# Attention scores in split fp32: two passes over the whole TensorE array in place of three passes of row pairs

## The chip, the core and the metric

The kernel runs on one core of a Trainium2 chip. The metric is the time of one execution on the device, in microseconds (us). The engines that matter here are TensorE (PE in the profile; PEld is its loading of stationary operands), VectorE (DVE), ScalarE (ACT) and SyncE (SP), which issues nearly all DMAs.

## The reference, cut to what matters

Two layers of a decoder trunk over 256 tokens of width 1024, all in fp32. Each layer has two attention mixers side by side and a feed-forward part. Three products of queries and keys, all with 64-wide heads, decide the scores:

```python
# DSA: an indexer scores all keys; the best 64 per token are kept
rel = jax.nn.relu(jnp.einsum('bthd,bsd->bths', iq_i, ik).astype(jnp.float32))
score = jnp.einsum('bths,bth->bts', rel, iw_i.astype(jnp.float32))
_, sel = lax.top_k(score, k_top)
...
s = jnp.einsum('bthd,btkhd->bhtk', q_i, kg) * ATTN_SCALE
...
# NSA: 8 heads in 2 groups; compressed, selected and window branches
s_s = jnp.einsum('bgrtd,bgtnkd->bgrtnk', q_i, kg)
s_w = jnp.einsum('bgrtd,bsgd->bgrts', q_i, kw) * ATTN_SCALE
...
x = x + _hybrid_mixer(...)
x = x + _swiglu(_rmsnorm(x, ffn_norm[l]), w_ffn_gate[l], w_ffn_up[l], w_ffn_down[l])
```

## The kernel before

**Split fp32.** A matmul in type f32r takes one pass, but keeps fewer bits than f32. So an fp32 value is held as a high part (rounded to f32r by ACT) and a low part (the value less its high part, by DVE), and a product of two fp32 values is three f32r matmuls: high by high, high by low, low by high. Weights go through `weights` (L155 to L167: a DMA, ACT at L164, DVE at L165) and `mul3` (L169 to L175); the activations are split once per norm.

**Scores.** One head has 64 rows, so it fills half of the array's 128 rows. Two heads (or groups) e = 0, 1 lie on rows 0 to 63 and 64 to 127 (`HALF`). `split` makes the high and low part of all 128 rows in one ACT and one DVE instruction. `pair` (L320 to L325) then issues, for each of the three products, one matmul on the upper and one on the lower 64 rows, each into a PSUM bank of its own. Per layer there are ten such blocks: two of the indexer for the second half of the tokens (256 keys wide, tiles `iqs`, `iks`), two of `nsa(0)` (256 wide) and four of `nsa(1)` (512 wide; tiles `qs`, `ks`), and two of `dsa(1)` (256 wide; tiles `dqs`, `dks`). A block of 256 columns is twelve matmuls, one of 512 columns six. The indexer and `dsa` for the first half of the tokens use plain f32 on row halves (L422, L648).

**Other tiled matmuls.** The values (L595, L636) use half of the array's columns, the compression (L505) a quarter. A plain f32 matmul shows as two in the trace.

**What sets the order.** The program is written layer by layer: indexer, NSA projections, compression, DSA projections, `nsa(0)`, `nsa(1)`, the splits of `dks` and `dqs` (L664 to L667), `dsa(0)`, `dsa(1)`, gate projections, branches, output, feed-forward. A list scheduler that simulates time then orders each engine's instructions; it mixes the attention's small matmuls into the projections that come before and after (their weights have buffers for four steps). Scores go to the two `sc` banks; both come free only when DVE has read them (L297, the first pass of `softmax`), so the next block waits for the softmax of the one before. `iks`, `ks` and `dqs` share one buffer (tag `ks`), `iqs`, `qs` and `dks` another (tag `qs`).

Of the kernel before, what the change touches and what calls it, by code (L numbers as in the profile page):

```python
# [9 lines left out]
F32 = mybir.dt.float32  # L10
F32R = mybir.dt.float32r
AF = mybir.ActivationFunctionType
# [4 lines left out]
P = 128  # L17
SEQ = 256
NT = SEQ // P
# [12 lines left out]
HALF = (slice(0, 64), slice(64, 128))  # L32
# [47 lines left out]
def hybrid_trunk(ctx: ExitStack, tc: tile.TileContext, a: dict, out: bass.AP):  # L80
    nc = tc.nc
# [5 lines left out]
    one = ctx.enter_context(tc.tile_pool(name="one", bufs=1))  # L87
# [224 lines left out]
        return pt  # L312


    def split(dst, src):

        nc.scalar.activation(dst[0], src, AF.Copy)
        nc.vector.tensor_sub(dst[1], src, dst[0].bitcast(F32))

    def pair(outs, q, k):  # L320


        for n, (a, b) in enumerate(((0, 0), (0, 1), (1, 0))):
            for e in range(2):
                nc.tensor.matmul(outs[e], q[a][HALF[e]], k[b][HALF[e]], start=n == 0, stop=n == 2)  # L325

    ALL = cst[:, K_ZERO:K_ZERO + 2 * P]

# [14 lines left out]
    for l in range(DEPTH):  # L343
# [14 lines left out]
        qT, dqT = carve(ga, 2608, 4, SEQ), carve(ga, 3632, 4, SEQ)  # L358
        accs = carve(ga, 4656, NT, SEQ)

        ks = one.tile([P, 2, NT, 2 * P], F32R, tag="ks", name="ks")
        qs = one.tile([P, 2, 4, SEQ], F32R, tag="qs", name="qs")
        ikT = carve(ga, 5168, P)
        gates = carve(gb, 0, NT, 2 * D)
# [1 line left out]
        dkT = carve(gb, 4096, 4, SEQ)  # L366
# [20 lines left out]
        iw = small.tile([P, NT, 8], F32, tag="iw", name="iw", bufs=1)  # L387
        dbias = []
        iqs = one.tile([P, 2, 4, SEQ], F32R, tag="qs", name="iqs")[:, :, :, 0:P]
        iks = one.tile([P, 2, NT, 2 * P], F32R, tag="ks", name="iks").rearrange("p a b t -> p a (b t)")[:, :, 0:SEQ]  # L390
        for i in range(NT):
            nc.vector.tensor_scalar_mul(iw[:, i], pji[:, i, 576:584], 512 ** -0.5)
            rope(pji[:, i, 0:576].rearrange("p (h d) -> p h d", d=64), i, (9,))
            nc.vector.tensor_copy(pji[:, i, 576:640], pji[:, i, 512:576])
            tok = slice(i * P, (i + 1) * P)
            qp = tr_bank()
            for k in range(4):
                nc.tensor.transpose(qp[:, k * P:(k + 1) * P], pji[:, i, k * P:(k + 1) * P], ident)
            q3 = qp.rearrange("p (k t) -> p k t", t=P)
            if i == 0:  # L400
                iqT = work.tile([P, 4, P], F32, tag="pr", name="iqT", bufs=8)
                nc.scalar.activation(iqT, q3, AF.Copy)
            else:
                split([iqs[:, a] for a in range(2)], q3)
            kp = tr_bank()[:, 0:P]
            nc.tensor.transpose(kp, pji[:, i, 512:640], ident)
            nc.scalar.activation(iks[:, 0, tok], kp, AF.Copy)
            if i == 0:
                nc.scalar.activation(ikT, kp, AF.Copy)
            nc.vector.tensor_sub(iks[:, 1, tok], kp, iks[:, 0, tok].bitcast(F32))  # L410
        for i in range(NT):
            nk = P * (i + 1)
            acc = accs[:, i, 0:nk]
            prev = causal(i)
            per = 512 // nk
            for p0 in range(0, 4, per):
                sbs = [sc_bank() for _ in range(2)]
                for p in range(p0, p0 + per):
                    outs = [sb[:, (p - p0) * nk:(p - p0 + 1) * nk] for sb in sbs]
                    if i == 0:  # L420
                        for e in range(2):
                            nc.tensor.matmul(outs[e], iqT[HALF[e], p], ikT[HALF[e]], start=True, stop=True)  # L422
                    else:
                        pair(outs, [iqs[:, z, p] for z in range(2)], [iks[:, z] for z in range(2)])
                for e in range(2):
                    rl = work.tile([P, 512], F32, tag="k2", name="rl", bufs=3)
                    nc.scalar.activation(rl, sbs[e], AF.Relu)
                    for p in range(p0, p0 + per):
                        h = 2 * p + e
                        nc.vector.scalar_tensor_tensor(acc, rl[:, (p - p0) * nk:(p - p0 + 1) * nk],  # L430
                                                       iw[:, i, h:h + 1], prev, ALU.mult, ALU.add)
                        prev = acc
            dbias.append(acc)
# [12 lines left out]
        for c0, n in ((512, 512), (1024, 280), (0, 512)):  # L446
            d = project(act, w_in, c0, n)
            for i in range(NT):
                if c0 == 0:
                    nq[i] = work.tile([P, 512], F32, tag="q2", name="nq", bufs=4)  # L450
                    evac(nq[i].rearrange("p (r g d) -> p r g d", r=4, g=2),
                         d[i].rearrange("p (g r d) -> p r g d", g=2, r=4), rstd[i])
                else:
                    evac(pj[:, i, c0 - C0:c0 - C0 + n], d[i][:, 0:n], rstd[i])
        eg = small.tile([P, NT, 24], F32, tag="eg", name="eg", bufs=1)
        kvP = work.tile([P, 2, 2, P], F32, tag="k2", name="kvP", bufs=3)
        for i in range(NT):
            rope(pj[:, i, 0:768].rearrange("p (a b d) -> p a b d", a=3, b=4)[:, :, 0:2], i, (3, 2))
            rope(nq[i].rearrange("p (h d) -> p h d", d=64), i, (8,))
            sp = tr_bank()  # L460
            for kind, c0 in ((0, C_KCMP), (1, C_VCMP)):
                for g in range(2):
                    for par in range(2):
                        o = (kind * 2 + g) * 64
                        nc.tensor.matmul(sp[par * 64:(par + 1) * 64, o:o + 64],
                                         pj[:, i, c0 - C0 + g * 64:c0 - C0 + g * 64 + 64],
                                         cst[:, K_SEL + par * 64:K_SEL + par * 64 + 64], start=True, stop=True)
            nc.vector.tensor_copy(kvP[:, :, :, i * 64:(i + 1) * 64],
                                  sp[:, 0:256].rearrange("p (k g c) -> p k g c", k=2, g=2))
            kp = tr_bank()  # L470
            for k, c in enumerate((C_KSLC, C_KWIN)):
                nc.tensor.transpose(kp[:, k * P:(k + 1) * P], pj[:, i, c - C0:c - C0 + P], ident)
            split([ks[:, z, i] for z in range(2)], kp[:, 0:2 * P])
            tok = slice(i * P, (i + 1) * P)
            qp = tr_bank()
            for r in range(4):
                nc.tensor.transpose(qp[:, r * P:(r + 1) * P], nq[i][:, r * P:(r + 1) * P], ident)
            q3 = qp.rearrange("p (r t) -> p r t", t=P)
            nc.scalar.activation(qT[:, :, tok], q3, AF.Copy)
            split([qs[:, z, :, tok] for z in range(2)], q3)  # L480
            nc.scalar.activation(eg[:, i], pj[:, i, C_NG - C0:C_NG - C0 + 24], AF.Exp, scale=-1.0)
            nc.vector.tensor_scalar(eg[:, i], eg[:, i], 1.0, None, ALU.add)

# [55 lines left out]
        for c0, dst in ((C_DQ, dqT), (C_DK, dkT), (C_DV, None)):  # L539
            d = project(act, w_in, c0, 512)  # L540
            for i in range(NT):
                if dst is None:
                    evac(dv[:, i], d[i], rstd[i])
                    continue
                q = work.tile([P, 512], F32, tag="q2", name="dq", bufs=4)
                evac(q, d[i], rstd[i])
                rope(q.rearrange("p (h d) -> p h d", d=64), i, (8,))
                transpose_into(dst[:, :, i * P:(i + 1) * P], [q[:, k * P:(k + 1) * P] for k in range(4)])
# [9 lines left out]
        def nsa(i):  # L558
# [42 lines left out]
            for r0 in range(0, 4, per):  # L601
# [1 line left out]
                sbs = [sc_bank() for _ in range(2)]  # L603
                outs = [[sb[:, n * 256 * (i + 1):(n + 1) * 256 * (i + 1)] for n in range(per)] for sb in sbs]
                for r in range(r0, r0 + per):
                    pair([o[r - r0] for o in outs], [qs[:, z, r, tok] for z in range(2)],
                         [ks[:, z, 0:i + 1].rearrange("p b t -> p (b t)") for z in range(2)])
                for g in range(2):
                    segs = []
                    for o in outs[g]:  # L610
# [14 lines left out]
        def dsa(i):  # L625
# [15 lines left out]
            for p0 in range(0, 4, per):  # L641
                pts = []
                sbs = [sc_bank() for _ in range(2)]
                for p in range(p0, p0 + per):
                    outs = [sb[:, (p - p0) * nk:(p - p0 + 1) * nk] for sb in sbs]
                    if i == 0:
                        for e in range(2):
                            nc.tensor.matmul(outs[e], dqT[HALF[e], p, 0:P], dkT[HALF[e], p, 0:P], start=True, stop=True)  # L648
                    else:
                        pair(outs, [dqs[:, z, p] for z in range(2)], [dks[:, z, p] for z in range(2)])  # L650
                for sb in sbs:
                    segs = sb.rearrange("p (h b t) -> p h b t", h=per, t=P)
                    pts.append(softmax([segs[:, h] for h in range(per)], dbias[i], None))
# [8 lines left out]
            nsa(i)  # L662

        dks = one.tile([P, 2, 4, SEQ], F32R, tag="qs", name="dks")  # L664
        dqs = one.tile([P, 2, NT, 2 * P], F32R, tag="ks", name="dqs").rearrange("p z b (c t) -> p z (b c) t", t=P)
        split([dks[:, z] for z in range(2)], dkT)
        split([dqs[:, z] for z in range(2)], dqT[:, :, P:])  # L667
        dsa(0)
        dsa(1)


# [187 lines left out]
```

## Time and profile before

| what | value |
|---|---|
| median of 3 runs | 834.9 us (834.82 to 835.3) |
| the profiled execution's own time | 835.01 us |
| its span in the trace | 833.0 us, 12280 instructions |
| mean granted TensorE clock | 0.999 of full speed |
| HBM read, written | 138.24 MB, 1.05 MB |

The time contains the span and some 2 us around it. Busy times of PE come from modelled ends: a matmul's record goes on past the start of the next one. So the pace of PE is read from the starts of successive rows, not from their durations.

### The profile page before, as it was taken

To read this page: it belongs to the slowest core of one execution; us is meant where nothing else is said; L and a number is where in the kernel's file an instruction comes from. 1 tells how busy PE (TensorE), PEld (TensorE's weight loads), DVE (VectorE), ACT (ScalarE), POOL (GpSimd) and SP (SyncE) were. 2 spreads that over 40 slices of the span, in tenths; PEclk is the share of its full clock that TensorE was granted. 3 is DMA by queue.
4 is the path that set the end of the run, shared out by engine and by line. 5 is a ranking of instruction groups with operands and counts; after the bars stand their busy time and mean duration, and the time that the engine had idled before them with its cause. 6 is when DMAs were issued, how large, how long until landed. Compare 5 with 4: busy or idle time off the path is not lost.

```text
span 833.0 us, 12280 instructions
## 1 busy us (share of the span) xinstructions
PE 824.6 (99%) x4501; PEld 680.1 (82%) x4501; DVE 534.0 (64%) x1163; ACT 452.4 (54%) x777; POOL 8.4 (1%) x18
## 2 busy tenths in 40 slices
PE   8999999999999999999999999999999999999997
PEld 7878887778888888988898888777788888889886
DVE  6699478868665556554668956767577555556445
ACT  6754467854565444533567545667546554544433
POOL 0100000000000000000000000000000000000000
PEclk9999999999999999999999999999999999999999
DMA  8955653225475664576376565332254755546651
GB/s 275 335 166 183 190 176 102 89 70 180 143 226 164 192 189 140 185 237 188 87 233 189 166 190 176 117 88 78 86 183 153 215 185 182 181 126 224 210 177 51
DMA packets 76331, 140.08 MB, mean 168 GB/s; under 512 B 5056, under 2 KB 24512, under 8 KB 76272
## 3 DMA queue, kind: packets, MB, share of 16 engines
q1 hardware_dynamic: 76032, 138.59, 53.5%
q0 software_dynamic: 240, 0.72, 0.4%
q8 instruction: 35, 0.57, 0.3%
q14 instruction: 24, 0.20, 0.1%
HBM read 138.24 MB, written 1.05 MB: 167 GB/s over the span
## 4 chain that ended last, share of the span: by engine, by line
PE 98%; DMA 1%; SPq 0%; ACT 0%; DVE 0%; issue 0%; POOLq 0%; ACTq 0%
PE mm L174 26%; PE mm L173 26%; PE mm L175 26%; PE sc L325 3%; PE tr L280 3%; PE yv L595 2%; PE sc L505 2%; PE yv L175 1%; PE yv L174 1%; PE yv L173 1%; PE tr L784 1%; PE yv L636 1%; DMA raw<-w_in 1%; PE tr L234 1%; PE yv L621 1%; PE sc L174 0%
## 5 line engine op out<-in xcount | busy, mean ns | idle before, releaser
L165 DVE TENSOR_TENSOR lo<-raw,hi 128x1024 fp32r<-128x1024 f32 (+3 forms) x264 | 302.2, 1149 | 174.6 <-ACT hi L164 170.4
L164 ACT ACTIVATE hi<-raw 128x1024 fp32r<-128x1024 f32 (+3 forms) x264 | 261.9, 999 | 209.4 <-PE mm L175 142.3
L174 PE MATMUL mm<-lo,ah 128*128 128x512 f32 (+3 forms) x850 | 319.9, 377 | 0.0
L173 PE MATMUL mm<-hi,ah 128*128 128x512 f32 (+3 forms) x850 | 318.7, 380 | 0.0
L175 PE MATMUL mm<-hi,al 128*128 128x512 f32 (+3 forms) x850 | 318.0, 376 | 0.0
L174 PEld LDWEIGHTS mm<-lo,ah 128*128 128x128 f32 x850 | 160.0, 188 | 29.4 <-issue 2.8
L175 PEld LDWEIGHTS mm<-hi,al 128*128 128x128 f32 x850 | 159.6, 188 | 28.7 <-issue 1.2
L173 PEld LDWEIGHTS mm<-hi,ah 128*128 128x128 f32 x850 | 159.7, 188 | 28.2 <-issue 0.7
L174 PE MATMUL mm<-lo,hh 128*128 128x512 f32 x126 | 49.3, 391 | 0.0
L175 PE MATMUL mm<-hi,hl 128*128 128x512 f32 x126 | 49.1, 390 | 0.0
L173 PE MATMUL mm<-hi,hh 128*128 128x512 f32 x126 | 48.7, 395 | 0.0
L300 ACT ACTIVATE pr<-pr,mx 128x128 f32<-128x128 f32 (+1 forms) x96 | 42.5, 445 | 10.4 <-DVE mx L297 10.3
L789 DVE TENSOR_TENSOR hl<-tr,hh 128x512 fp32r<-128x512 f32 (+1 forms) x24 | 15.5, 647 | 36.0 <-ACT hh L788 36.0
L788 ACT ACTIVATE hh<-tr 128x512 fp32r<-128x512 f32 (+1 forms) x24 | 13.5, 562 | 44.6 <-PE tr L784 44.6
L175 PEld LDWEIGHTS mm<-hi,hl 128*128 128x128 f32 x126 | 23.7, 188 | 4.9
L174 PEld LDWEIGHTS mm<-lo,hh 128*128 128x128 f32 x126 | 23.7, 188 | 4.1
L173 PEld LDWEIGHTS mm<-hi,hh 128*128 128x128 f32 x126 | 23.7, 188 | 4.1
L309 DVE TENSOR_SCALAR pr<-pr,c 128x128 f32<-128x128 f32 (+1 forms) x96 | 25.3, 316 | 1.0
L281 ACT COPY pt<-tr 128x512 f32<-128x512 f32 x36 | 20.4, 583 | 9.7 <-PE tr L280 9.6
L297 DVE CUSTOM_DVE_ANT_0 pr<-sc,cst 128x128 f32<-128x128 f32 (+1 forms) x64 | 19.1, 354 | 6.8 <-PE sc L325 6.8
L280 PE MATMUL tr<-cst,pr 128*128 128x128 f32 x144 | 22.3, 278 | 0.0
L775 ACT ACTIVATE sg<-mm,rstd 128x512 f32<-128x512 f32 (+1 forms) x24 | 15.7, 654 | 8.8 <-PE mm L175 8.6
(242 smaller groups left out, 777.2 us busy)
## 6 DMA issues: line engine op xcount, KB each, us to landing
raw<-w_in SPq DMA_DIRECT2D x72, 512.0 KB, 3.5
raw<-w_ffn_down SPq DMA_DIRECT2D x44, 512.0 KB, 4.4
raw<-w_ffn_gate SPq DMA_DIRECT2D x40, 512.0 KB, 4.2
raw<-w_ffn_up SPq DMA_DIRECT2D x40, 512.0 KB, 4.3
raw<-w_out SPq DMA_DIRECT2D x16, 512.0 KB, 3.5
raw<-w_in SPq DMA_DIRECT2D x16, 292.0 KB, 3.5
raw<-w_branch_nsa SPq DMA_DIRECT2D x16, 256.0 KB, 4.0
raw<-w_branch_dsa SPq DMA_DIRECT2D x8, 512.0 KB, 3.5
```

What stands on the lines that cost most here:

```text
L164: nc.scalar.activation(hi[:, 0:kt * n], raw[:, 0:kt * n], AF.Copy)
L165: nc.vector.tensor_sub(lo[:, 0:kt * n], raw[:, 0:kt * n], hi[:, 0:kt * n].bitcast(F32))
L173: nc.tensor.matmul(dst, xh, wh, start=first, stop=False)
L174: nc.tensor.matmul(dst, xh, wl, start=False, stop=False)
L175: nc.tensor.matmul(dst, xl, wh, start=False, stop=last)
L280: nc.tensor.transpose(tp[:, k * P:(k + 1) * P], piece, ident)
L281: nc.any.tensor_copy(dst, tp[:, 0:len(parts) * P].rearrange("p (k t) -> p k t", t=P))
L297: nc.vector.tensor_tensor_reduce(pr[:, h].rearrange("p (b t) -> p b t", t=P), v, b3, -0.125, 3.4e38, ALU.add, ALU.min, accum_out=mx[:, h:h ...
L300: nc.scalar.activation(pr[:, h], pr[:, h], AF.Exp, bias=mx[:, h:h + 1], scale=-1.0, accum_out=sm[:, h:h + 1])
L309: nc.vector.tensor_scalar_mul(pr[:, h], pr[:, h], c[:, h:h + 1])
L325: nc.tensor.matmul(outs[e], q[a][HALF[e]], k[b][HALF[e]], start=n == 0, stop=n == 2)
L505: nc.tensor.matmul(hp[q:q + 32, 0:P], blk[:, half * 8 + mq * 4 + m], w1[:, m], start=mq == 0 and m == 0, stop=mq == 1 and m == 3, tile_pos ...
```

## The change

For scores the sum over a head's 64 rows now uses all 128 rows of the array. One side of the product holds its high part on one half of the rows and its low part on the other half (`stack`: two ACT and two DVE instructions, each over 64 rows, where `split` had one and one; DVE writes the low part to the other half). The other side holds its high part on both halves, in one tile, and its low part on both halves, in a second tile (`twice`: eight instructions over 64 rows, of which two are copies that the scheduler may give to any engine, where `split` had two). `score` then multiplies the stacked side with the high tile and with the low tile: two matmuls on all 128 rows for each head, where `pair` took three on 64 rows. Low by low, which was left out, is now added too. The tag `ks` doubles in size, and the pool tag `q2` goes from four to three buffers.

```diff
-    def split(dst, src):
-        nc.scalar.activation(dst[0], src, AF.Copy)
-        nc.vector.tensor_sub(dst[1], src, dst[0].bitcast(F32))
-
-    def pair(outs, q, k):
-        for n, (a, b) in enumerate(((0, 0), (0, 1), (1, 0))):
-            for e in range(2):
-                nc.tensor.matmul(outs[e], q[a][HALF[e]], k[b][HALF[e]], start=n == 0, stop=n == 2)
+    def stack(dst, src):
+        for e in range(2):
+            nc.scalar.activation(dst[e][HALF[e]], src[HALF[e]], AF.Copy)
+        for e in range(2):
+            nc.vector.tensor_sub(dst[e][HALF[1 - e]], src[HALF[e]], dst[e][HALF[e]].bitcast(F32))
+
+    def twice(dh, dl, src):
+        for e in range(2):
+            nc.scalar.activation(dh[e][HALF[e]], src[HALF[e]], AF.Copy)
+            nc.any.tensor_copy(dh[e][HALF[1 - e]], src[HALF[e]])
+        for e in range(2):
+            for h in (e, 1 - e):
+                nc.vector.tensor_sub(dl[e][HALF[h]], src[HALF[e]], dh[e][HALF[e]].bitcast(F32))
+
+    def score(o, q, k):
+        pairs = [(q, t) for t in k] if isinstance(k, (list, tuple)) else [(t, k) for t in q]
+        for n, (u, v) in enumerate(pairs):
+            nc.tensor.matmul(o, u, v, start=n == 0, stop=n == 1)
...
-        ks = one.tile([P, 2, NT, 2 * P], F32R, tag="ks", name="ks")
+        ks = one.tile([P, 4, NT, 2 * P], F32R, tag="ks", name="ks")
+        kh, kl = [ks[:, g] for g in range(2)], [ks[:, 2 + g] for g in range(2)]
...
-                split([iqs[:, a] for a in range(2)], q3)
+                stack([iqs[:, e] for e in range(2)], q3)
...
-                        pair(outs, [iqs[:, z, p] for z in range(2)], [iks[:, z] for z in range(2)])
+                        for e in range(2):
+                            score(outs[e], iqs[:, e, p], [iks[:, z] for z in range(2)])
...
-                    nq[i] = work.tile([P, 512], F32, tag="q2", name="nq", bufs=4)
+                    nq[i] = work.tile([P, 512], F32, tag="q2", name="nq", bufs=3)
...
-            split([ks[:, z, i] for z in range(2)], kp[:, 0:2 * P])
+            twice([t[:, i] for t in kh], [t[:, i] for t in kl], kp[:, 0:2 * P])
...
-            split([qs[:, z, :, tok] for z in range(2)], q3)
+            stack([qs[:, g, :, tok] for g in range(2)], q3)
...
-                    pair([o[r - r0] for o in outs], [qs[:, z, r, tok] for z in range(2)],
-                         [ks[:, z, 0:i + 1].rearrange("p b t -> p (b t)") for z in range(2)])
+                    for g in range(2):
+                        score(outs[g][r - r0], qs[:, g, r, tok],
+                              [t[g][:, 0:i + 1].rearrange("p b t -> p (b t)") for t in (kh, kl)])
...
-                        pair(outs, [dqs[:, z, p] for z in range(2)], [dks[:, z, p] for z in range(2)])
+                        for e in range(2):
+                            score(outs[e], [dqs[:, z, p] for z in (e, 2 + e)], dks[:, e, p])
...
-        split([dks[:, z] for z in range(2)], dkT)
-        split([dqs[:, z] for z in range(2)], dqT[:, :, P:])
+        stack([dks[:, e] for e in range(2)], dkT)
+        twice([dqs[:, e] for e in range(2)], [dqs[:, 2 + e] for e in range(2)], dqT[:, :, P:])
```

The change also gives the scheduler other lengths and other dependences, so it orders the instructions anew. Three places follow. The rows are the engine's instructions in program order (line, operation, written tile and read tiles, shape, count); lines of the changed kernel are its own (L335 is `score`, L318 and L320 are `stack`, L325, L326 and L329 are `twice`, L607 and L649 are the values that were L595 and L636).

TensorE in the second layer, `nsa(0)`, the scores of two banks. Before, the six matmuls of one bank's half stood apart from the six of the next:

```order
L175 MATMUL mm<-hi,al 128x512
L325 MATMUL sc<-ks,qs 128x256 x6
L173 MATMUL mm<-hi,ah 128x512
L174 MATMUL mm<-lo,ah 128x512
L325 MATMUL sc<-ks,qs 128x256 x6
L175 MATMUL mm<-hi,al 128x512
L280 MATMUL tr<-cst,pc 128x128
```

In the change the same stage has:

```order
L175 MATMUL mm<-hi,al 128x512
L173 MATMUL mm<-hi,ah 128x512
L335 MATMUL sc<-ks,qs 128x256 x8
L174 MATMUL mm<-lo,ah 128x512
L175 MATMUL mm<-hi,al 128x512
L173 MATMUL mm<-hi,ah 128x512
```

Two runs of six have become one run of eight. Over the whole program L325 has 192 matmuls in 29 rows before, and L335 has 128 in 31 rows; the values (L595 and L636, then L607 and L649) stand in 33 rows before and in 22 now, and the compression (L505) gains two separate runs.

TensorE in the second layer, `nsa(1)`, the second of its four blocks of 512 columns. Before:

```order
L621 MATMUL yv<-pct,gb 128x128 x4
L280 MATMUL tr<-cst,pr 128x128 x4
L325 MATMUL sc<-ks,qs 128x512 x5
L280 MATMUL tr<-cst,pr 128x128 x4
L325 MATMUL sc<-ks,qs 128x512
L174 MATMUL mm<-lo,ah 128x512
```

In the change:

```order
L335 MATMUL sc<-ks,qs 128x512
L280 MATMUL tr<-cst,pr 128x128 x4
L607 MATMUL yv<-pt,ga 64x128 x8
L335 MATMUL sc<-ks,qs 128x512 x2
L280 MATMUL tr<-cst,pc 128x128
L335 MATMUL sc<-ks,qs 128x512
L173 MATMUL mm<-hi,ah 128x512
```

The block is still cut into pieces by transposes and values, in other places.

VectorE in the first layer, between the last softmax of `nsa(1)` (L297 reading `cst`) and the first of `dsa(0)` (L297 reading `ga`). Before:

```order
L297 ISA pr,mx<-sc,cst 128x256
L297 ISA mx 128x1
L318 TENSOR_TENSOR dks<-gb,dks 128x1024
L318 TENSOR_TENSOR dqs<-ga,dqs 128x512
L165 TENSOR_TENSOR lo<-raw,hi 128x1024
L305 SCALAR_TENSOR_TENSOR sm<-sm,eg 128x2
```

In the change:

```order
L297 ISA pr,mx<-sc,cst 128x256
L297 ISA mx 128x1
L326 CAST dqs<-ga 64x512 x2
L320 TENSOR_TENSOR dks<-gb,dks 64x1024 x2
L329 TENSOR_TENSOR dqs<-ga,dqs 64x512 x4
L305 SCALAR_TENSOR_TENSOR sm<-sm,eg 128x2
L297 ISA pr,mx<-sc,ga 128x128
```

Two DVE instructions have become eight, each over half of the rows and as many columns as before; both copies of this `twice` went to DVE, and the first softmax of `dsa(0)` follows right behind. The same stands in the second layer.

## Rows read from the trace of the kernel before

**Rows 1.** The page: busy time by engine; the chain that ended last, by engine.

```profile
PE 824.6 (99%) x4501; PEld 680.1 (82%) x4501; DVE 534.0 (64%) x1163; ACT 452.4 (54%) x777; POOL 8.4 (1%) x18
PE 98%; DMA 1%; SPq 0%; ACT 0%; DVE 0%; issue 0%; POOLq 0%; ACTq 0%
```

**Rows 2.** Busy time in one stretch of the attention of the first layer.

```profile
150.00:165.00 15.00, 15.00 (x112) 11.46 (x112) 13.01 (x54) 12.68 (x37) 0.00 (x0) 1.00 0.21 70
```

**Rows 3.** Source view of L325, tiles `ks`, `qs` (duration ns min/median/max, starts, forms).

```profile
L325 PE MATMUL sc<-ks,qs x96: 275/384/502, 114.0 to 563.1; 64*128 64x256 f32 x48, 64*128 64x512 f32 x48
```

**Rows 4.** Timeline of PE, a block of twelve (columns: start us, us, instruction, count).

```profile
48.29 0.39 PE L175 MATMUL mm<-hi,al 128*128 128x512 f32 x1
48.52 0.39 PE L173 MATMUL mm<-hi,ah 128*128 128x512 f32 x1
48.83 0.98 PE L325 MATMUL sc<-iks,iqs 64*128 64x256 f32 x12
49.74 0.50 PE L174 MATMUL mm<-lo,ah 128*128 128x512 f32 x1
50.08 0.39 PE L175 MATMUL mm<-hi,al 128*128 128x512 f32 x1
```

**Rows 5.** Timeline of PE, six scores of one half alone.

```profile
521.86 0.39 PE L175 MATMUL mm<-hi,al 128*128 128x512 f32 x1
522.17 0.97 PE L325 MATMUL sc<-ks,qs 64*128 64x256 f32 x6
523.08 0.50 PE L173 MATMUL mm<-hi,ah 128*128 128x512 f32 x1
523.41 0.40 PE L174 MATMUL mm<-lo,ah 128*128 128x512 f32 x1
```

**Rows 6.** Timeline of PE, a block of 512 columns.

```profile
146.73 0.98 PE L325 MATMUL sc<-ks,qs 64*128 64x512 f32 x6
147.63 0.50 PE L174 MATMUL mm<-lo,ah 128*128 128x512 f32 x1
```

**Rows 7.** Timeline of PE, the first and last of twelve whole-array matmuls of 256 columns.

```profile
825.35 0.28 PE L173 MATMUL sc<-hi,hh 128*128 128x256 f32 x1
...
826.67 0.28 PE L175 MATMUL sc<-spare,hl 128*128 128x256 f32 x1
```

**Rows 8.** Timeline of PE, the first and last of the 29 runs of L325.

```profile
41.97 0.38 PE L325 MATMUL sc<-iks,iqs 64*128 64x256 f32 x1
...
584.31 0.97 PE L325 MATMUL sc<-dks,dqs 64*128 64x256 f32 x6
```

**Rows 9.** Timeline of PE, a short run on half of the columns.

```profile
541.22 0.39 PE L174 MATMUL mm<-lo,ah 128*128 128x512 f32 x1
541.54 0.43 PE L595 MATMUL yv<-pt,ga 128*64 128x128 f32 x2
541.90 0.50 PE L175 MATMUL mm<-hi,al 128*128 128x512 f32 x1
542.24 0.39 PE L174 MATMUL mm<-lo,ah 128*128 128x512 f32 x1
```

**Rows 10.** Source view of the low parts that `split` makes (L318).

```profile
L318 DVE TENSOR_TENSOR ks<-tr,ks x4: 420/427/447, 57.8 to 479.8; 128x256 fp32r<-128x256 f32 x4
L318 DVE TENSOR_TENSOR qs<-tr,qs x4: 682/688/714, 64.0 to 482.7; 128x512 fp32r<-128x512 f32 x4
L318 DVE TENSOR_TENSOR iqs<-tr,iqs x2: 684/688/692, 38.0 to 442.0; 128x512 fp32r<-128x512 f32 x2
L318 DVE TENSOR_TENSOR dks<-gb,dks x2: 1219/1220/1221, 155.6 to 564.7; 128x1024 fp32r<-128x1024 f32 x2
L318 DVE TENSOR_TENSOR dqs<-ga,dqs x2: 684/684/684, 156.7 to 565.8; 128x512 fp32r<-128x512 f32 x2
```

**Rows 11.** Timelines of DVE and PE: the last scores of `dsa(0)` read; the first of `dsa(1)`.

```profile
161.31 0.09 DVE L297 DVE_READ_ACCUMULATOR2_ANT mx<- 128x1 f32 x1
...
166.39 0.97 PE L325 MATMUL sc<-dks,dqs 64*128 64x256 f32 x12
```

More of the change, by code (lines that the diff above doesn't have):

```diff
@@ L389, in hybrid_trunk @@
         iqs = one.tile([P, 2, 4, SEQ], F32R, tag="qs", name="iqs")[:, :, :, 0:P]
-        iks = one.tile([P, 2, NT, 2 * P], F32R, tag="ks", name="iks").rearrange("p a b t -> p a (b t)")[:, :, 0:SEQ]
+        iks = one.tile([P, 4, NT, 2 * P], F32R, tag="ks", name="iks").rearrange("p a b t -> p a (b t)")[:, 0:2, 0:SEQ]
         for i in range(NT):
@@ L544, in hybrid_trunk @@
                     continue
-                q = work.tile([P, 512], F32, tag="q2", name="dq", bufs=4)
+                q = work.tile([P, 512], F32, tag="q2", name="dq", bufs=3)
                 evac(q, d[i], rstd[i])
@@ L664, in hybrid_trunk @@
         dks = one.tile([P, 2, 4, SEQ], F32R, tag="qs", name="dks")
-        dqs = one.tile([P, 2, NT, 2 * P], F32R, tag="ks", name="dqs").rearrange("p z b (c t) -> p z (b c) t", t=P)
-        split([dks[:, z] for z in range(2)], dkT)
-        split([dqs[:, z] for z in range(2)], dqT[:, :, P:])
+        dqs = one.tile([P, 4, NT, 2 * P], F32R, tag="ks", name="dqs").rearrange("p z b (c t) -> p z (b c) t", t=P)
+        stack([dks[:, e] for e in range(2)], dkT)
+        twice([dqs[:, e] for e in range(2)], [dqs[:, 2 + e] for e in range(2)], dqT[:, :, P:])
         dsa(0)
```

## The prediction, as put on record before the changed kernel ran

> **What bounds the kernel now.** I read the page first: PE is busy for 824.6 of 833.0 us, and 98% of the chain that ended last lies on PE [rows 1]. DVE has 299 us idle and ACT 381, so what the change adds there costs nothing until PE waits for it, and what it takes from PE is gained nearly one to one, as long as other work stands ready. Busy PE is not PE at its best, so the second view is PE's timeline, read by starts. Between whole-array matmuls of 512 columns the step is 0.23 us (48.29 to 48.52) [rows 4]; over many rows it is 0.227. The reader is to see what a block of scores does to this rhythm. From the last full matmul (48.52) to the first score pass 0.31 us; twelve scores on row halves take 0.91 us (48.83 to 49.74); and the first full matmul behind them is followed by the next only after 0.34 [rows 4]. Going from the whole array to halves and back costs (0.31 - 0.23) + (0.34 - 0.23), about 0.2 us outside the block, and something inside it. How much inside shows in the comparison with six scores of one half alone: they take 0.91 us too (522.17 to 523.08) [rows 5]. So two halves do run side by side, and six matmuls that find no partner cost as much as twelve that do. Six paired ones of 512 columns take 0.90 us as well (146.73 to 147.63) [rows 6].
>
> A whole-array matmul of 256 columns steps by 0.120 us: from the first to the twelfth 1.32 us, eleven steps [rows 7].
>
> **The scores, before.** There are 192 of them, 48 with 512 columns [rows 3] and so 144 with 256, in 29 runs from 41.97 to 584.31 [rows 8]. Taken run by run from the timeline, from the first score of a run to the next other matmul, they hold PE for 24.5 us, 0.845 us a run (most are 0.90; cut pieces of one to five are 0.31 to 0.66; two with badly paired halves 1.14 and 1.25). To each belongs the 0.2 us of going in and out: 29 x 0.2 = 5.8. Seven runs stand right behind a value run (L595), which would pay its own way out, some 0.1 us each, without them: -0.7. Sum **29.6 us**.
>
> **The scores, after.** 128 whole-array matmuls: 96 x 0.120 + 32 x 0.227 = 11.5 + 7.3 = **18.8 us**, with no change of shape before or behind them, wherever the scheduler cuts them. The price is nearly exact, since both widths occur in the trace in the same type on the whole array [rows 4, 7]. Gain **10.8 us**. It does not come from fewer columns: paired perfectly, with changes of shape for nothing, six pairs of 256 would be 0.72 us against 0.96 for eight full ones.
>
> At this point the Trainium skill speaks against the change: "TensorEngine Tiling (Array Packing)", section Overview, gives up to twice the speed for contractions of 64 or fewer rows. Its section Key Properties says that changing the tiling mode drains TensorE. Here rows 4 to 6 agree with both sentences, and the second weighs more in blocks this short.
>
> **Other changes of shape.** The order of PE is new. The value runs go from 33 to 22, and the compression gains two. One run costs, besides its own matmuls, 0.32 - 0.23 on the way in and 0.34 - 0.23 behind it, and about 0.1 more in its last step (two matmuls took 0.36 where the pace is some 0.1 each) [rows 9]: 0.3 us. That is 11 x 0.3 - 2 x 0.3 = 2.7 us at most. Some of the runs that vanish stood directly beside a score run, whose entry I have counted already, so I take **2.0**; the ends are 0 and 2.7.
>
> **DVE and ACT.** The half-height instructions do not occur before. I bound the price of one by half of the full-height row below (half the rows) and by twice that row above (source and target on different halves), and take the full-height price itself, since in the rows the duration follows the columns: 0.427 us at 256, 0.688 at 512, 1.220 at 1024 [rows 10]. Per layer DVE then gets, more than before: indexer 0.69; `ks` twice 3 x 0.43 and one copy 0.43, 3.0; `qs` 2 x 0.69 = 1.4; `dks` 1.22; `dqs` 3 x 0.684 and two copies, bounded by 0.684 each, 3.4. Sum 9.7 us, 19.4 for both layers; ACT gets ten instructions more per layer, about half of that time. All of it is hidden by PE's own work where results are needed late: the parts of `ks` and `qs` are made from 58 us on and first used at 114, and the indexer's, made at 38.0, first at 41.97, 3.3 us after they are done [rows 3, 8, 10]. The same holds for the smaller pool `q2`: the tiles of one projection are transposed while PE does the next, 48 matmuls or 10.9 us.
>
> One place is short: between `nsa(1)` and `dsa(1)`. There DVE goes from 1.220 + 0.684 = 1.90 us to 2 x 1.220 + 6 x 0.684 = 6.54 at most, 4.6 more, and DVE is busy for 13.01 of 15 us in that stretch [rows 2]. Queued behind on DVE are the first softmax of `dsa(0)`, which frees the two score banks, and the low parts of weights; PE waits for the banks with the scores of `dsa(1)`. Before, the banks were read at 161.40 and the scores started at 166.39 [rows 11]: 5.0 us of slack, of which 0.4 would be left. PE comes there a little earlier than before, having saved the changes of shape in between. So I allow **0.5 us of waiting per layer, 1.0 in all**; the ends are 0 and, at twice the price, what the second rival says.
>
> **Sum.** -10.8 - 2.0 + 1.0 = -11.8. The profiled execution took 835.01, 0.1 more than the median of 834.9; 835.01 - 11.8 = 823.2. With the other ends: 835.01 - 10.8 - 2.7 = 821.5, and 835.01 - 10.8 + 1 = 825.2.
>
> **Rivals.** *One, part of the gain is given back by DVE.* If half-height instructions that cross halves cost 1.4 times a full-height one, the 6.54 us are 9.2, the burst is 7.3 us longer, 5.0 are hidden, and PE waits 2.3 us in each layer: with the 1.0 left out, 835.01 - 12.8 + 4.6 = 826.8. At twice the price it is 13.1, 11.2 longer, 6.2 per layer, and 834.6: no difference. For it speaks that DVE has little room there [rows 2]; against it that the added instructions have no more columns than those known.
>
> *Two, the pairs were the cheaper way* (the other side). If the 0.2 us around a run and the unpaired sixes came back in another shape, because the new score runs fall beside value runs and transposes and stay cut up, only the columns would count: twelve blocks of 256 go from 6 to 8 steps of 0.120, 2.9 us more, eight of 512 from 3 to 4 steps of 0.227, 1.8 more: 839.7. It decides from about 39 changes of shape and back more than I count (11.8 us at 0.3 each). By the rule on small contractions alone, from the page named above, this would be the outcome. Against it stand the 0.91 us of six lone matmuls [rows 5] and the new order, where 25 of 31 score runs stand between whole-array matmuls.
>
> *Three, it does not do what it says*: the order shows 128 matmuls instead of 192, so this is out.
>
> **How the numbers follow.** 0.2% (1.7 us) is about what a measurement of this kernel can tell from no change. Forecast, 820 to 825.5: 0.70. First rival, up to 833: 0.18, and up to no difference 0.05. Second rival: 0.05, and 0.02 for a slower end of the first. So 823.2 is the prediction; 820 to 830 leaves out the upper part of the first rival, the second, and little below. Faster 0.88, the same 0.05, slower 0.07.
>
> **What would show it.** Right: L335 in steps of 0.12 and 0.227 us with no gap around; runs of 0.48 us where there were 0.91; PE's busy share still 99%; DVE some 19 us and ACT about half of that busier. Wrong: PE idle, or steps far over 0.23, ended by DVE before the scores of `dsa(1)`, with L320, L326 and L329 longer than 0.43, 0.69 and 1.22; or steps of 0.3 us and more on either side of L335. If the gain is larger, it is in the other runs, not in the scores.

## The result and the profile after

The changed kernel takes 820.94 us (median of 4 runs, 820.89 to 821.11) against 834.91 (834.82 to 835.3): a ratio of 0.9832 with a 95% interval of [0.9815, 0.9849]. The forecast was 823.2 in 820 to 830. The profiled execution took 821.0 us with a span of 819.2, at a mean granted clock of 0.999 of full speed (2.4 GHz); the span is 13.8 us shorter than before.

The page of the changed kernel, busy time by engine and the chain that ended last by engine (answers to [rows 1]):

```profile
span 819.2 us, 12201 instructions
PE 810.9 (99%) x4437; PEld 679.2 (83%) x4437; DVE 549.5 (67%) x1201; ACT 461.3 (56%) x791; POOL 8.4 (1%) x18
PE 98%; DMA 1%; SPq 0%; ACT 0%; DVE 0%; issue 0%; POOLq 0%; ACTq 0%
```

PE is as much the bound as before. DVE is busy for 15.5 us more and ACT for 8.9, and none of it shows in the chain.

PE's timeline of the changed kernel: an undivided block of 256 columns for both heads (answers to [rows 4, 5]) and four matmuls of 512 (answers to [rows 6]):

```profile
521.13 0.39 PE L173 MATMUL mm<-hi,ah 128*128 128x512 f32 x1
521.35 1.12 PE L335 MATMUL sc<-ks,qs 128*128 128x256 f32 x8
522.31 0.40 PE L174 MATMUL mm<-lo,ah 128*128 128x512 f32 x1
522.54 0.40 PE L175 MATMUL mm<-hi,al 128*128 128x512 f32 x1
...
548.77 1.17 PE L335 MATMUL sc<-ks,qs 128*128 128x512 f32 x4
549.78 0.40 PE L175 MATMUL mm<-hi,al 128*128 128x512 f32 x1
```

Read by starts: 0.22 us from the last full matmul to the block, 0.96 for eight matmuls (0.120 each), and 0.23 from the first full matmul behind it to the second. Nothing is left of the 0.31 and 0.34 of [rows 4]. Four of 512 columns take 1.01 us, 0.1 more than four times 0.227; they stand behind transposes, the last of which takes 0.03 us there in place of its usual 0.11, so next to nothing is lost.

The same accounting by starts over the whole trace shows where the 13.8 us came from. Each matmul's time runs to the start of the next matmul, so what a run costs on its way in and in its second step behind is booked on its neighbours:

| PE, start to start, us | before | after |
|---|---|---|
| scores (L325, L335) | 24.51 in 29 runs | 20.15 in 31 runs |
| products with weights | 702.07 | 697.45 |
| transposes | 48.72 | 46.48 |
| values (L595 and L636, L607 and L649) | 23.17 in 33 runs | 20.27 in 22 runs |
| compression (L505, L517) | 13.70 in 8 runs | 14.34 in 10 runs |
| f32 scores of `dsa(0)` | 2.51 | 2.18 |

With the in and out booked back on them, the scores cost 29.56 us before and 19.22 after: **-10.3**. Where a score run stands beside a value run, the share of each is a choice; other choices move each of the two sums by up to 0.4, and their difference by 0.2. The rest of the span, -3.5, is in the other lines.

### The profile page after: what moved, and what is told of

Its sections match the earlier page's. It is cut to its first block, busy times and chain, and to the rows that moved or that the text cites. A ratio compares the mean times of both kernels' runs of the same rounds, so it can differ in the third digit from the quotient of the medians.

```text
span 819.2 us, 12201 instructions
## 1 busy us (share of the span) xinstructions
PE 810.9 (99%) x4437; PEld 679.2 (83%) x4437; DVE 549.5 (67%) x1201; ACT 461.3 (56%) x791; POOL 8.4 (1%) x18
## 4 chain that ended last, share of the span: by engine, by line
PE 98%; DMA 1%; SPq 0%; ACT 0%; DVE 0%; issue 0%; POOLq 0%; ACTq 0%
PE mm L175 26%; PE mm L173 26%; PE mm L174 26%; PE tr L280 3%; PE sc L335 2%; PE sc L517 2%; PE yv L607 2%; PE yv L175 2%; PE yv L174 2%; PE yv L173 1%; PE tr L798 1%; PE yv L649 1%; DMA raw<-w_in 1%; PE tr L234 1%; PE yv L634 1%; PE sc L174 0%
## 5 line engine op out<-in xcount | busy, mean ns | idle before, releaser
L803 DVE TENSOR_TENSOR hl<-tr,hh 128x512 fp32r<-128x512 f32 (+1 forms) x24 | 15.5, 647 | 36.5 <-ACT hh L802 36.5
L297 DVE CUSTOM_DVE_ANT_0 pr<-sc,cst 128x128 f32<-128x128 f32 (+1 forms) x64 | 19.0, 353 | 6.3 <-PE sc L335 6.0
L789 ACT ACTIVATE sg<-mm,rstd 128x512 f32<-128x512 f32 (+1 forms) x24 | 15.7, 654 | 8.8 <-PE mm L175 8.6
L281 ACT COPY pt<-tr 128x512 f32<-128x512 f32 x32 | 17.6, 584 | 4.4 <-PE tr L280 4.4
```

The costliest lines, as they stand in the source:

```text
L281: nc.any.tensor_copy(dst, tp[:, 0:len(parts) * P].rearrange("p (k t) -> p k t", t=P))
L297: nc.vector.tensor_tensor_reduce(pr[:, h].rearrange("p (b t) -> p b t", t=P), v, b3, -0.125, 3.4e38, ALU.add, ALU.min, accum_out=mx[:, h:h ...
```

## The experiments

Theory A is the prediction's: a matmul costs its columns, and a run on part of the array costs a fixed price for the change of shape. Its rivals are B (only the number of matmuls counts), C (the gain is only the new order of everything else) and D (DVE's new work gives back part of the gain). Medians are in us; each ratio is to the kernel before on the same chip, which took 834.6 to 834.9.

### The third product put back on the whole array

```diff
-        for n, (u, v) in enumerate(pairs):
-            nc.tensor.matmul(o, u, v, start=n == 0, stop=n == 1)
+        for n, (u, v) in enumerate(pairs[:1] + pairs):
+            nc.tensor.matmul(o, u, v, start=n < 2, stop=n != 1)
```

The changed kernel, with the first product issued twice: 192 whole-array matmuls.

> The changed kernel with its first score matmul issued twice (the second starts the sum anew), so that scores are again 192 matmuls, all on the whole array. Theory A (the gain is the changes of shape and the badly paired halves, at some 0.2 to 0.3 us for each run): 48 x 0.120 + 16 x 0.227 = 9.4 us more than the changed kernel, 830.3 us, still 4.6 below the kernel before with the same number of score matmuls. Theory B (the gain is that a third of the score matmuls is gone): all of it is lost, 834.9.

833.8 (832.5 to 836.27), 0.9988 [0.9978, 0.9997]. PE's timeline, an undivided block of twelve:

```profile
119.70 0.39 PE L175 MATMUL mm<-hi,al 128*128 128x512 f32 x1
119.92 1.60 PE L335 MATMUL sc<-ks,qs 128*128 128x256 f32 x12
121.36 0.40 PE L173 MATMUL mm<-hi,ah 128*128 128x512 f32 x1
121.59 0.40 PE L174 MATMUL mm<-lo,ah 128*128 128x512 f32 x1
```

Twelve take 1.44 us with clean steps on both sides, and the score rows of the whole trace grow from 20.15 to 29.73, +9.6 where A's prices give 9.4. So the prices hold. But the scores then cost 28.9 us, hardly less than the 29.56 of the row pairs: with three products the whole array alone brings next to nothing, and the time is nearer to B's 834.9 than to A's 830.3. The 3.5 us by which it is above A's number are outside the scores: PE waited 1.4 us at the end of the attention for ACT (L567), which it did not in the changed kernel, and the rows of values are 2.2 us longer (24 runs in place of 22).

### Two products on row halves

```diff
-        for n, (a, b) in enumerate(((0, 0), (0, 1), (1, 0))):
+        for n, (a, b) in enumerate(((0, 0), (0, 1))):
...
-                nc.tensor.matmul(outs[e], q[a][HALF[e]], k[b][HALF[e]], start=n == 0, stop=n == 2)
+                nc.tensor.matmul(outs[e], q[a][HALF[e]], k[b][HALF[e]], start=n == 0, stop=n == 1)
```

The kernel before without its third product (low by high is left out): 128 matmuls, as after the change.

> The kernel before with row pairs, but only two of the three products (low by high is left out of the scores), so that there are 128 score matmuls as in the changed kernel, on row halves. Theory A (runs and changes of shape): every run loses one step of a pair, about 29 x 0.23 = 6.7 us, and the value runs fall from 33 to 26, 2.1 us: 826.1; the whole array keeps an advantage of 5 us at the same number of products. Theory B (the number of score matmuls): 820.9.

828.1 (828.0 to 829.26), 0.9925 [0.9911, 0.994]: 2.0 above A's number, and 7.2 above the changed kernel with the same number of matmuls, so B alone is out. (The profiled execution is the one of 829.26: PE waited 1.7 us for ACT before the first products with weights, which is far from the scores.) PE's timeline, an undivided block of eight:

```profile
120.09 0.39 PE L173 MATMUL mm<-hi,ah 128*128 128x512 f32 x1
120.41 0.75 PE L325 MATMUL sc<-ks,qs 64*128 64x256 f32 x8
121.09 0.50 PE L174 MATMUL mm<-lo,ah 128*128 128x512 f32 x1
121.42 0.40 PE L175 MATMUL mm<-hi,al 128*128 128x512 f32 x1
```

The four kernels now give a table. The price of one undivided 256-column block for both heads is the time from the last full matmul ahead of it to the second behind, less two ordinary steps (0.454): [rows 4] 0.31 + 0.91 + 0.34 - 0.454 = 1.11; here 0.32 + 0.68 + 0.33 - 0.454 = 0.87. "All undivided" takes 12 such blocks and 8 of 512 columns (for pairs, 1.10 with three products and 0.87 with two, by the same reading; for the whole array, 1.36 and 0.91, by 0.227 a step).

| scores, us | one block | all undivided | as measured in the trace | lost to cutting | median |
|---|---|---|---|---|---|
| row pairs, three products (before) | 1.11 | 22.1 | 29.6 | 7.5 | 834.9 |
| whole array, three products | 1.44 | 28.2 | 28.9 | 0.7 | 833.8 |
| row pairs, two products | 0.87 | 17.4 | 25.2 | 7.8 | 828.1 |
| whole array, two products (the change) | 0.96 | 18.8 | 19.2 | 0.4 | 820.9 |

Undivided, pairs are the cheaper way at the same number of products, 0.87 against 0.96 and 1.11 against 1.44. But blocks do not stay undivided. The scheduler cuts them, the two banks come free at different times, and matmuls of one half stand alone. Pairs pay 7.5 us for that, the whole array next to nothing. Of the gain of 10.3, then, 3.3 us is the block's own price (22.1 - 18.8), and 7.0 us is what cutting no longer costs. The medians add that the change needs both of its halves: against the kernel before on the same chip, two products alone bring 6.5 us, the whole array alone 1.0, both together 14.0.

### One product at a time

The kernel before with the new form in the indexer alone, in NSA alone and in `dsa(1)` alone.

```diff
-                stack([iqs[:, e] for e in range(2)], q3)
+                split([iqs[:, a] for a in range(2)], q3)
...
-                        for e in range(2):
-                            score(outs[e], iqs[:, e, p], [iks[:, z] for z in range(2)])
+                        pair(outs, [iqs[:, z, p] for z in range(2)], [iks[:, z] for z in range(2)])
```

(Seen from the changed kernel, this is how one of the three goes back to pairs.)

> Only the indexer's scores by two whole-array passes, NSA and DSA by row pairs as before. Theory A, from the runs of the kernel before: 5.4 us with their changes of shape become 32 x 0.120 = 3.8, 1.5 less, 833.4; the value runs stay 33. Theory C (the gain is the new order of everything else): no relation to the block's own price, anything within 10 us.

> Only the scores of NSA by two whole-array passes. Theory A: 18.0 us of the runs of before become 32 x 0.120 + 32 x 0.227 = 11.1, 6.9 less; value runs from 33 to 28, 1.5 less: 826.5. Theory C: no relation to these sums.

> Only the scores of dsa(1) by two whole-array passes. Theory A: 6.2 us become 3.8, 2.4 less; value runs from 33 to 27, 1.8 less: 830.7. Theory C: no relation to these sums. With e2 and e3 the score parts add up to the 10.8 us of the prediction.

Indexer alone 832.74, 0.9975 [0.9965, 0.9985]; NSA alone 825.86, 0.9893 [0.9878, 0.9908]; `dsa(1)` alone 830.48, 0.9945 [0.993, 0.9959]. All three are within 0.7 us of what was expected, which C does not explain. For NSA alone part of that is luck: 2.2 us of its gain lie in the scores of `dsa(1)`, which were not expected to move, while PE waited 1.3 us more than before (for ACT, L577) and the rows of values did not get shorter (23.17 and 23.08) though 1.5 were expected. The gains add to 2.2 + 9.1 + 4.4 = 15.7, 1.7 more than the whole. A part is counted twice: with NSA alone changed, the pairs of `dsa(1)` already fell from 6.23 to 4.03 us, because the new order no longer split them.

### Both score banks as one

```diff
+    def sc_banks():
+        t = ps.tile([P, 2, 512], F32, tag="sc", name="sc", bufs=1)
+        return [t[:, 0], t[:, 1]]
...
-                sbs = [sc_bank() for _ in range(2)]
+                sbs = sc_banks()
```

The kernel before, with both banks one tile, so that they come free together and each half finds its partner.

> The kernel before, its two score banks allocated as one tile, so that both halves of a block become free together; its order has 25 score runs instead of 29, no six of one half alone, and 30 value runs instead of 33. Theory A: four times 1.1 us for the eight lone sixes that are paired, 1.5 for pieces that are whole again, 0.9 for the value runs: 6.8 less, 828.1, more where a block now waits for both banks. Theory B: the number of matmuls is that of before, so no difference, 834.9.

842.4 (841.64 to 844.26), 1.0091 [1.0076, 1.0106]: A's number was missed by 14 us, on the other side. The blocks did get cheaper, 24.51 to 19.89 us by starts in 25 runs, but both banks now wait for the whole softmax. Waits of PE (us in total, times, longest):

```profile
PE sc L329 <- DVE mx L301: 3.2, 3, 2.1
PE tr L284 <- DVE pr L313: 2.4, 2, 2.1
```

Two windows of it (granted clock behind the busy times):

```profile
174.00:178.00 4.00, 1.90 (x31) 1.63 (x28) 4.00 (x26) 2.83 (x15) 0.00 (x0) 1.00 0.01 2
178.00:182.00 4.00, 3.50 (x20) 2.31 (x17) 3.86 (x22) 2.38 (x10) 0.00 (x0) 0.56 0.00 0
```

PE is busy for 1.90 of 4 us, and then runs with a mean granted clock of 0.56, that is, for most of the stretch at its lower level of 1.2 GHz. The lower clock does not explain the median, though: an execution of this kernel with a mean clock of 0.999 took 841.6. By the waits, two banks that come free apart were worth more than whole pairs.

### The order of the halves

```diff
-        for n, (a, b) in enumerate(((0, 0), (0, 1), (1, 0))):
-            for e in range(2):
+        for e in range(2):
+            for n, (a, b) in enumerate(((0, 0), (0, 1), (1, 0))):
```

The kernel before, with three matmuls of one half issued before three of the other, meant to take pairing away altogether.

> The kernel before with the three products of one half issued ahead of the three of the other, so that halves rarely find a partner. If two halves run side by side (theory A): six lone steps of 0.120 more in each block of 256 columns that was paired (about eight), 5.8, and three of 0.235 in each of the eight blocks of 512, 5.6: some 10 us more, 845. If halves never ran side by side: no difference, 834.9.

832.72 (832.46 to 832.93), 0.9972 [0.9961, 0.9983], a miss. PE's timeline of a block of 512 columns, both halves:

```profile
134.44 0.43 PE L595 MATMUL yv<-pt,ga 128*64 128x128 f32 x2
134.80 0.98 PE L325 MATMUL sc<-ks,qs 64*128 64x512 f32 x6
135.71 0.50 PE L174 MATMUL mm<-lo,ah 128*128 128x512 f32 x1
```

Six take 0.91 us as in [rows 6], where one after the other they would be 6 x 0.227 = 1.36. Their starts come in pairs, 0.01 us apart or less, as in the kernel before. So halves run side by side in either order of issue, and the experiment did not remove what it was meant to remove (the scores cost 30.2 us, 29.56 before). The gain of 2.2 us is in the rest and goes with five value runs fewer (33 to 28).

The mirror of it in the changed kernel lets the two heads take turns, which on the whole array should change nothing:

```diff
+        for n in range(2):
+            for o, q, k in zip(outs, qs, ks):
+                u, v = (q, k[n]) if isinstance(k, (list, tuple)) else (q[n], k)
+                nc.tensor.matmul(o, u, v, start=n == 0, stop=n == 1)
```

> The changed kernel with its score matmuls written in another order (the two heads take turns), the same instructions otherwise. The scores keep their price (19 us); the order has 26 value runs instead of 22. Theory A: 4 x 0.3 = 1.2 us more, 822.1. How far it lies from 820.9 is how much the scheduler's order alone is worth.

823.14 (823.0 to 823.32), 0.9863 [0.9848, 0.9878]. The scores cost 19.5 us, as in the changed kernel; the 2.2 us more go with 26 value runs instead of 22. So order alone moved the kernel before by 2.2 us down and the changed one by 2.2 us up.

### DVE's new work doubled

```diff
-            nc.vector.tensor_sub(dst[e][HALF[1 - e]], src[HALF[e]], dst[e][HALF[e]].bitcast(F32))
+            for _ in range(2):
+                nc.vector.tensor_sub(dst[e][HALF[1 - e]], src[HALF[e]], dst[e][HALF[e]].bitcast(F32))
...
-            for h in (e, 1 - e):
+            for h in (e, 1 - e, e, 1 - e):
```

In the changed kernel every low part is computed twice, first for all products, then only for those of the indexer and NSA.

> The changed kernel with every low part of stack and twice made twice, 19 us more on DVE, of which 5.2 us in each layer between nsa(1) and dsa(1). Theory A (TensorE alone bounds, DVE is hidden): 821 to 822. Rival D (there is next to no room at that place): up to 4.8 us of waiting in each layer, 826 to 831.

> As e5 (low parts made twice on DVE), but only those of the indexer and of NSA, 14 us more on DVE in all, none between nsa(1) and dsa(1). If only that place has no room: 821 to 822. If DVE has no room anywhere in the attention: a good part of the 15 us that e5 lost, 828 or more.

All doubled: 836.45 (833.89 to 838.28), 1.0016 [1.0005, 1.0028]. Early ones only: 823.82 (823.23 to 824.11), 0.9869 [0.9853, 0.9886]. Waits of PE with all doubled:

```profile
PE sc L336 <- DVE c L307: 1.9, 2, 0.9
...
PE sc L336 <- DVE mx L297: 1.2, 1, 1.2
PE sc L336 <- DVE dqs L330: 0.7, 2, 0.3
```

Windows of the same kernel from the scores of `dsa(1)` on:

```profile
170.00:174.00 4.00, 2.31 (x9) 1.46 (x9) 3.92 (x14) 1.94 (x9) 0.00 (x0) 0.96 0.17 18
174.00:176.00 2.00, 2.00 (x15) 1.57 (x14) 1.92 (x11) 0.80 (x4) 0.00 (x0) 0.50 0.61 227
176.00:178.00 2.00, 2.00 (x14) 1.88 (x13) 0.66 (x3) 0.22 (x1) 0.00 (x0) 0.72 0.02 6
```

D's mechanism exists, at the place that was forecast, but D's number (826 to 831) was exceeded by more than 5 us. All of the gain was lost, 15.5 us, 12.6 of them only once `dks` and `dqs` are doubled too. PE waited 8 us longer in all than in the changed kernel: 3.8 of it before and between the scores of `dsa(1)` (the lines above), the rest mostly behind them, for low parts of weights (1.3) and for ACT at the end of the attention (1.7). Behind the waits its clock fell: (1 - granted) over these three windows is 0.16 + 1.0 + 0.56 = 1.7 us, and the second layer has the same stretch. Some 4 us of the 15.5 are not accounted for by these two. Doubling the early parts cost 2.9 us, more than the 0 to 1 expected: 1.4 of it is waits, and the rest goes with 26 value runs in place of 22.

### The compression on the whole array

```diff
-                        nc.tensor.matmul(hp[q:q + 32, 0:P], blk[:, half * 8 + mq * 4 + m], w1[:, m],
-                                         start=mq == 0 and m == 0, stop=mq == 1 and m == 3, tile_position=(0, q))
...
+                        nc.tensor.matmul(hp[:, kind * 32:(kind + 1) * 32], w1[:, m], blk[:, half * 8 + mq * 4 + m],
+                                         start=half + mq + m == 0, stop=half == 1 and mq == 1 and m == 3)
```

A try to go on from the changed kernel: weights and activations change sides, and the runs on a quarter of the columns vanish.

> The changed kernel with the compression's matmuls on the whole array too (weights stationary, 32 columns moving, the same number of matmuls; the sum over quarters and its copy fall away). Theory A: ten runs on a quarter of the columns no longer change the shape, 10 x 0.3 = 3.0 us, and four matmuls less, 0.3: 817.6. Theory B (number of matmuls): 820.6.

821.27 (819.54 to 822.42), 0.9833 [0.9817, 0.9849]: equal to the changed kernel, and 3.7 above A's 817.6. A wait of PE in the profiled execution (822.42 us), in total and in the first layer:

```profile
PE sc L517 <- DMA w<-cmpv_w: 1.7, 2, 1.0
...
89.29 1.08 PE L517 MATMUL sc<-blk,w 128*128 128x32 f32 x8 [0.95 <-DMA w<-cmpv_w]
```

Two windows there:

```profile
88.00:90.00 2.00, 1.04 (x11) 0.81 (x8) 1.74 (x2) 0.74 (x2) 0.00 (x0) 1.00 0.55 108
90.00:92.00 2.00, 2.00 (x11) 1.81 (x11) 1.05 (x5) 0.70 (x2) 0.00 (x0) 0.57 0.88 266
```

The changes of shape are gone, and the rows of the compression are 0.7 us shorter (14.34 to 13.66) though they hold this wait. PE now comes to `cmpv_w` before its DMA has landed: it waits 1.0 us in the first layer, behind which the clock falls to a mean of 0.57 in the next window, and 0.7 in the second, behind which it does not fall. The two executions with a mean clock of 0.999 took 819.5 and 820.6. No experiment beat the changed kernel by its median.

## Why the prediction was right, point by point

**The scores, -10.8: measured -10.3.** Both sums held: 29.6 before (29.56 by the trace) and 18.8 after (19.22). The prices of 0.120 and 0.227 held to some 0.1 us a run. Two readings beside the first sum were slightly off and do not change it: six score runs stand right behind a value run, not seven, and the cut pieces of five take 0.88 and 0.90 us, not at most 0.66. What the prediction did not split is where the gain is: the smaller part in the block's own price, the larger in that a whole-array run may be cut anywhere.

**Other changes of shape, -2.0: measured -3.5, beyond the end of 2.7.** This is the term that was most off. The step that failed is the price of a run, "0.3 us". [Rows 4] give 1.11 - 6 x 0.120 = 0.39 us besides the matmuls' own steps, and the block of eight above 0.87 - 4 x 0.120 = 0.39 again. In the short value run I had counted some 0.1 inside, taking 0.1 as the pace of each of its two rows; in the long value runs the two rows of one f32 matmul take 0.11 together, so [rows 9] hold 0.36 - 0.11 = 0.25 inside and 0.2 outside, 0.45 in all. Nine runs fewer (33 to 22, and 8 to 10) are 3.5 us at 0.39 and 4.1 at 0.45. That the first of these meets the measured rest is partly chance: runs that stand side by side share a way in or out, and the price of a compression run was not read by itself. What the table above shows directly is 2.9 us less in the rows of values, 0.6 more in the compression and 0.3 less in `dsa(0)`; about 0.9 more lies in the steps beside them. The two experiments in which only the order moved agree in size: five value runs fewer, -2.2 us; four more, +2.2. The number of runs is the scheduler's doing, though; the change only gave it other lengths and dependences.

**Waiting, +1.0: measured 0.** The whole list of PE's waits in the changed kernel, none of them in the attention:

```profile
PE tr L112 <- DVE warm L118: 1.2, 1, 1.2
PE sc L174 <- DVE lo L165: 0.5, 2, 0.3
PE sc L173 <- ACT hi L164: 0.5, 1, 0.5
```

The source view of the new instructions (answers to [rows 10]) shows how near the estimate of their price was:

```profile
L320 DVE TENSOR_TENSOR qs<-tr,qs x8: 683/690/694, 64.3 to 481.4; 64x512 fp32r<-64x512 f32 x8
L320 DVE TENSOR_TENSOR dks<-gb,dks x4: 1218/1220/1221, 155.8 to 559.8; 64x1024 fp32r<-64x1024 f32 x4
...
L329 DVE TENSOR_TENSOR ks<-tr,ks x16: 407/422/428, 57.7 to 480.3; 64x256 fp32r<-64x256 f32 x16
L329 DVE TENSOR_TENSOR dqs<-ga,dqs x8: 683/686/689, 158.2 to 563.1; 64x512 fp32r<-64x512 f32 x8
...
L326 DVE CAST dqs<-ga x4: 420/422/423, 154.9 to 558.1; 64x512 fp32r<-64x512 f32 x4
```

Half the rows cost as much as all of them, 0.690 against 0.688 and 1.220 against 1.220, also where the target is the other half. Only the copies were cheaper, 0.422 where 0.684 was the bound. Timelines of DVE and PE between `nsa(1)` and `dsa(1)` (answers to [rows 11]):

```profile
154.91 0.85 DVE L326 CAST dqs<-ga 64x512 fp32r<-64x512 f32 x2
155.78 2.45 DVE L320 TENSOR_TENSOR dks<-gb,dks 64x1024 fp32r<-64x1024 f32 x2
158.25 2.79 DVE L329 TENSOR_TENSOR dqs<-ga,dqs 64x512 fp32r<-64x512 f32 x4
...
162.84 0.08 DVE L297 DVE_READ_ACCUMULATOR2_ANT mx<- 128x1 f32 x1
...
165.84 1.21 PE L335 MATMUL sc<-dks,dqs 128*128 128x256 f32 x8
```

The burst is 6.1 us long (154.91 to 161.04), the banks are read at 162.92 and the scores start at 165.84. So 2.9 of the 5.0 us of slack are left, not 0.4: the burst is 0.4 shorter than bounded, begins 0.7 earlier than the first row of `dks` in [rows 10], and the `lo` of 1.2 us and some 1.1 us of the softmax's small instructions, which stood ahead of the last read, now come after it; PE for its part comes 0.55 earlier (165.84 against 166.39). The prediction took the 5.0 us for both layers. In the second layer the slack before was only 3.9 (banks read at 571.43, scores at 575.33), less than the 4.6 us that it added; there, too, 2.9 were left after (565.69 to 568.61), for the same reasons.

**DVE's growth, 19.4: measured 15.5**, and ACT's 8.9, "about half" as said. The new instructions alone, counts times medians of the source views against [rows 10], are 18.3 us more, the four copies of `dqs` making the difference to 19.4. Busy time counts overlapping records once. Added up record by record, DVE's work grew by 20.9: besides the 18.3 there are 4.1 from six copies of `pt` and `ga` that the scheduler gave to DVE in place of ACT, and 1.5 less elsewhere.

**The sum, -11.8: measured -13.8 by the span.** The waiting that did not come (1.0) and the other changes of shape (1.5) make it larger, the scores (0.5) smaller. So 820.94 lies below the best case that the prediction added up, 821.5, and the range, down to 820, held it by 0.9 us: by its margin and not by its working. The prediction did say where a larger gain would lie, in the other runs and not in the scores.

**The rivals.** The first (DVE gives back) did not happen, but it is real and not far: its room is in the 2.9 us before `dsa(1)`, and the doubled parts went past it. The second (pairs cheaper) is wrong for this kernel, though its premise holds at the same number of products: undivided, pairs are 0.09 and 0.33 us cheaper a block. With three products against two, as here, even the undivided pair block is 0.15 dearer (1.11 and 0.96). The Trainium skill, "TensorEngine Tiling (Array Packing)", has both halves of it, the gain in its Overview and the drain at a change of mode under Key Properties. The traces agree with both and give the price: at 0.39 us a run, 29 runs cost 11.3 us, more than the whole gain in the scores. By B the two kernels with 128 matmuls would have been equal; they are 7.2 us apart.

**What stays open.** How the 3.5 us divide between the change and the scheduler's chance order was not separated beyond the two order runs; an order alone was worth 2.2. Some 4 us of the doubled DVE run are not accounted for.

## What to carry to other kernels

Price a tiled matmul by its run, not by its columns: about 0.4 us a run here, besides its own steps, as much as three whole-array steps of 256 columns; and count the runs in the order that the scheduler really makes. If short blocks are mixed into other work, use the idle rows for another part of the same sum (here high and low) in place of a second head: two full passes can be cut anywhere and need no partner. Test the two halves of such a change apart: here neither fewer products nor the whole array alone brought even half of the 14.0 us. Before spending work on an engine that is off the path, find the one place where the path waits for it soon after, and measure the slack there.

## What the runs showed of the hardware that was not expected

- Matmuls on two row halves run side by side even when three of one half are issued before three of the other: they start in pairs, and six of 512 columns take 0.91 us.
- In the profiled executions of four experiments the granted clock fell to its lower level soon after PE had waited: after a single wait of 1.0 us (the compression on the whole array; 0.57 in the window shown), after 0.9, 0.3 and 0.7 in quick succession (DVE's work doubled; 0.50), after 2.1 (both banks as one; 0.56) and after 1.7 (two products on row halves; 0.50 from 8 to 10 us). So a wait can cost more than itself. It does not always: no fall followed the 0.7 us in the second layer of the compression's run, and other executions of that kernel and of the one with both banks as one ran at a mean of 0.999. What decides it is not shown.
- DVE's subtraction costs by columns here: 64 rows cost what 128 do, and writing to the other half costs nothing extra.
